# Half B's last gate and up products as 2x2 blocks: seven block products in place of eight

## The chip, the cores and the metric

The kernel runs on one core of a Trainium2 chip, as one launch. The metric is the device time of a run in microseconds (us); lower is better. A core has five engines that run their own queues in order and meet at semaphores: PE (TensorE, matmuls; PEld is its weight load), DVE (VectorE), ACT (ScalarE), POOL (GpSimd) and SP (SyncE), from whose queue the DMAs of this kernel are issued. SBUF is the on-chip memory of 128 partitions, PSUM the memory of eight banks into which PE writes.

## The reference

Two layers work on 1088 tokens of 1024 channels: 1024 of a prompt, 64 of a running stream. Layer 0 mixes tokens by two recurrences (an RWKV-7 state and a gated linear attention), layer 1 by attention over the own chunk of 64 tokens and the eight before it. After each comes a layer norm, then a channel mixer and another layer norm:

```python
def swiglu(x, w_in, w_out):
    gate, up = jnp.split(x @ w_in, 2, axis=-1)
    return (jax.nn.silu(gate) * up) @ w_out

x = layer_norm(DEEPNORM_ALPHA * x + mix, P['ln1_w'][layer], P['ln1_b'][layer])
x = layer_norm(DEEPNORM_ALPHA * x + swiglu(x, P['ffn_w_in'][layer], P['ffn_w_out'][layer]),
               P['ln2_w'][layer], P['ln2_b'][layer])
```

`FFN_HIDDEN` is 2816, so `x @ w_in` has 5632 columns, 2816 of gate and 2816 of up. Everything is fp32, and the outputs are the two sequences and the states.

## The kernel before, in words

The tokens are two halves: A with 448 (384 of the prompt and the 64 of the stream), B with the other 640. Every stage exists once per half, and stages of the two halves are interleaved, so that PE has matmuls while the other engines work on the other half. A scheduler of the framework sets the order of each engine's queue from the program, its dependencies and its own estimate of the times; pools of a fixed number of buffers (`bufs`) set how far work can run ahead.

Precision comes from splitting: a value is kept as a high part `hi` (fp32r) and a low part `lo` (what the rounding left), and a product of two split values takes three matmuls, hi*hi, hi*lo and lo*hi. `split` (L108) makes both from an fp32 source, the high part by a copy on ACT (L110), the low part by a subtraction on DVE (L111). `load_w` (L91) does the same for a weight tile of 512 KB: DMA into `wr` (two buffers), cast on ACT (L98) into `wh`, low part into `wl`, in the later stages 5/8 on DVE (L103) and 3/8 on POOL (L105); `wh` and `wl` have four buffers each.

`layer_norm` (L847) works on one tile of 128 tokens at a time: statistics and scaling on DVE, ACT and POOL (L861 to L874), then eight transposes on PE (L879) into two PSUM banks of four blocks, and a split of each bank into `xt`, the normalised tokens with channels on the partitions: `xh` and `xl`, eight blocks of 128 channels by 640 tokens for half B. `proj` (L840) is the product ahead of that norm, and calls it for each token tile.

`ffn` (L891) is the channel mixer. It goes over 22 hidden tiles `j` of 128. For each it loads the gate's and the up's weights (`w_fi`, eight blocks of 128x128 each), and `gemm_ws` (L113) makes for each of them and for both segments of 320 tokens 24 matmuls of 320 columns: 96 for a tile. Three PSUM banks (`bank`, L136) turn round. Tanh on ACT (L903) and two steps on DVE (L904, L908) give silu(gate) * up, which is split into `hh` and `hl` (L912, L914). After the 4th, 8th, 12th, 16th, 18th and 22nd hidden tile `tsg` (L792) multiplies those hidden tiles with the output weights (`w_fo`) and adds to the token accumulators `acc` on DVE (L814, L816). With the last group each finished token tile goes through its layer norm.

`run` (L1162) strings this together. Near the end `proj` and the first layer norm of half B in layer 1 run within half A's mixer (after its hidden tile 20); then follows the rest of half A's mixer with its last layer norm, whose tiles go out to memory; then half B's mixer and last norm, to the end.

## Time and profile before

| | us |
|---|---|
| median of three runs | 3122.81 (3121.77 to 3125.4) |
| profiled execution | 3121.55 |
| its span, first to last instruction | 3119.8 |
| half B's first norm of layer 1, from its statistics on | 2588.27 |
| first gate matmul of half B's last mixer | 2646.90 |
| last matmul | 3108.2 |

The profile is of one execution. A row of a timeline has the start in us, the duration in us, engine, source line, operation and the tiles written and read, then in brackets the engine's idle time ahead of it and what ended that. A row of a grouped view has the summed duration and the mean in ns. The view of stretches has for each engine the busy time and the count of instructions, then the clock granted to PE as a share of the full one, the DMA share and GB/s. Matmul ends are modelled and overlap, so the distance between starts is their rate.

### The profile page before, as it was taken

The page shows a single profiled execution, that of the slowest core. Times are in us where ns is not written, and L with a number is a line of the kernel's source. Part 1 is how long each engine was busy: PE and PEld are TensorE (multiplying, and loading weights), DVE is VectorE, ACT ScalarE, POOL GpSimd, SP SyncE. Part 2 cuts the span into 40 slices and gives each one's busy share as a digit, 9 for nine tenths or more (in the row PEclk, how much of TensorE's full clock was granted, in tenths as well). Part 3 has the DMA queues.
Part 4 walks back from the last instruction along what each step waited for, and adds up shares of the span by engine and source line. Part 5 has one row for each costly group of instructions (what it writes and reads, how often), then busy time and mean ns, then how long its engine had stood idle before and what let it go on. Part 6 is the DMA issues. An engine that isn't in the chain of part 4 may idle for free.

```text
span 3119.8 us, 50207 instructions
## 1 busy us (share of the span) xinstructions
PE 3038.1 (97%) x17732; PEld 2705.3 (87%) x17732; DVE 1898.4 (61%) x4786; ACT 1208.7 (39%) x2657; POOL 1228.6 (39%) x1373
## 2 busy tenths in 40 slices
PE   8999999799999999999999999999999999999998
PEld 7788888688888878888999898899999988999997
DVE  5677875878899764375554466254666668433345
ACT  4454554344454323334442132354444442222221
POOL 2354533444455233343342233244455544222222
PEclk9989999889999999999999999999999999999999
DMA  6554434533533238534442233866454543322221
GB/s 208 139 156 113 109 110 122 147 103 106 148 109 107 87 104 270 179 99 125 119 129 92 81 95 104 249 185 185 132 142 136 148 140 108 106 81 69 82 75 68
DMA packets 297338, 395.10 MB, mean 127 GB/s; under 512 B 125376, under 2 KB 218424, under 8 KB 297088
## 3 DMA queue, kind: packets, MB, share of 16 engines
q1 hardware_dynamic: 297088, 391.90, 42.3%
q8 instruction: 140, 2.29, 0.3%
q14 instruction: 110, 0.90, 0.1%
HBM read 319.44 MB, written 75.51 MB: 127 GB/s over the span
## 4 chain that ended last, share of the span: by engine, by line
PE 83%; DVE 8%; DMA 5%; issue 2%; ACT 1%; POOL 1%; SPq 1%; POOLq 0%; DVEq 0%; ACTq 0%
PE gps L121 14%; PE gps L122 14%; PE gps L123 14%; PE gps L131 8%; PE gps L132 8%; PE gps L134 8%; PE op L1150 2%; PE tp L1124 2%; PE sps L1108 1%; DVE t L541 1%; DVE x L543 1%; PE sps L1109 1%; PE ps L614 1%; DVE wl L103 1%; PE pb L476 1%
## 5 line engine op out<-in xcount | busy, mean ns | idle before, releaser
L121 PE MATMUL gps<-xh,wh 128*128 128x320 f32 (+1 forms) x2892 | 963.0, 333 | 8.2 <-ACT xh L207 5.9
L122 PE MATMUL gps<-xl,wh 128*128 128x320 f32 (+1 forms) x2892 | 961.9, 333 | 0.6 <-DVE xl L208 0.6
L123 PE MATMUL gps<-xh,wl 128*128 128x320 f32 (+1 forms) x2892 | 959.2, 332 | 1.0 <-DVE wl L103 0.9
L105 POOL TENSOR_TENSOR wl<-wr,wh 128x384 fp32r<-128x384 f32 (+2 forms) x333 | 577.3, 1738 | 904.6 <-ACT wh L98 859.0
L98 ACT CAST wh<-wr 128x1024 fp32r<-128x1024 f32 x396 | 413.2, 1048 | 707.4 <-issue 234.9
L121 PEld LDWEIGHTS gps<-xh,wh 128*128 128x128 f32 x2892 | 545.7, 189 | 30.2 <-ACT xh L207 5.9
L123 PEld LDWEIGHTS gps<-xh,wl 128*128 128x128 f32 x2892 | 545.0, 188 | 19.5 <-DVE wl L103 2.1
L122 PEld LDWEIGHTS gps<-xl,wh 128*128 128x128 f32 x2892 | 545.2, 189 | 18.4 <-DVE xl L208 1.0
L103 DVE TENSOR_TENSOR wl<-wr,wh 128x640 fp32r<-128x640 f32 (+2 forms) x333 | 319.2, 959 | 339.8 <-ACT wh L98 338.0
L1119 POOL TENSOR_SCALAR s<-s,mx 128x640 f32<-128x640 f32 (+5 forms) x144 | 203.0, 1410 | 289.0 <-DVE mx L1118 249.6
L131 PE MATMUL gps<-wh,hh 128*128 128x512 f32 x792 | 313.0, 396 | 0.6 <-DVE acc L816 0.6
L132 PE MATMUL gps<-wl,hh 128*128 128x512 f32 x792 | 311.6, 395 | 0.0
L134 PE MATMUL gps<-wh,hl 128*128 128x512 f32 x704 | 274.3, 395 | 2.6 <-DVE hl L914 2.6
L816 DVE TENSOR_TENSOR acc<-acc,gps 128x512 f32<-128x512 f32 (+1 forms) x216 | 145.2, 681 | 105.9 <-PE gps L134 100.5
L134 PE MATMUL gps<-wh,xl 128*128 128x512 f32 (+1 forms) x441 | 175.9, 403 | 4.8 <-DVE xl L208 4.8
L131 PE MATMUL gps<-wh,xh 128*128 128x512 f32 (+1 forms) x441 | 176.0, 405 | 4.3 <-DVE acc L814 3.5
L132 PE MATMUL gps<-wl,xh 128*128 128x512 f32 (+1 forms) x441 | 176.6, 403 | 2.8 <-DVE wl L103 2.8
L131 PEld LDWEIGHTS gps<-wh,hh 128*128 128x128 f32 x792 | 149.2, 189 | 32.4 <-DVE acc L816 3.3
L541 DVE TENSOR_TENSOR t<-lt,x 16x48 f32<-16x48 f32 (+9 forms) x540 | 151.0, 280 | 40.7 <-DMA lt<-l_d 30.3
L908 DVE SCALAR_TENSOR_TENSOR ht<-ht,gps 128x320 f32<-128x320 f32 (+1 forms) x132 | 69.8, 529 | 173.8 <-PE gps L123 173.7
L132 PEld LDWEIGHTS gps<-wl,hh 128*128 128x128 f32 x792 | 149.3, 189 | 29.1 <-DVE wl L103 0.3
L1117 ACT ACTIVATE s<-s,mx 128x640 f32<-128x640 f32 (+5 forms) x144 | 96.5, 670 | 178.7 <-DVE mx L1116 174.8
(288 smaller groups left out, 4945.3 us busy)
## 6 DMA issues: line engine op xcount, KB each, us to landing
wr<-in_w_fi SPq DMA_DIRECT2D x176, 512.0 KB
wr<-in_w_fo SPq DMA_DIRECT2D x88, 512.0 KB
wr<-in_w_in SPq DMA_DIRECT2D x44, 512.0 KB
wr<-in_w_qk SPq DMA_DIRECT2D x32, 512.0 KB
qs<-qd SPq DMA_DIRECT2D x32, 320.0 KB
wr<-in_w_om SPq DMA_DIRECT2D x16, 512.0 KB
wr<-in_w_v SPq DMA_DIRECT2D x16, 512.0 KB
vd<-vh SPq DMA_DIRECT2D x16, 512.0 KB
```

The costliest lines, as they stand in the source:

```text
L98: self.A.copy(hi, raw)
L103: self.V.tensor_tensor(lo[:, :h], raw[:, :h], hi[:, :h].bitcast(F32), op=ALU.subtract)
L105: self.G.tensor_tensor(lo[:, h:], raw[:, h:], hi[:, h:].bitcast(F32), op=ALU.subtract)
L121: self.T.matmul(ps, hi[:, kt, :], xh, start=(kt == 0), stop=False)
L122: self.T.matmul(ps, hi[:, kt, :], xl, start=False, stop=False)
L123: self.T.matmul(ps, lo[:, kt, :], xh, start=False, stop=(kt == nk - 1))
L131: self.T.matmul(ps, hi(kt)[:, cols], wh, start=(i == 0), stop=False)
L132: self.T.matmul(ps, hi(kt)[:, cols], wl, start=False, stop=(lo is None and i == n - 1))
L134: self.T.matmul(ps, lo(kt)[:, cols], wh, start=False, stop=(i == n - 1))
L541: V.tensor_tensor(tv, lt[:, j, w:16].unsqueeze(2).to_broadcast([m, r, w]), x[:, 0, j, 0:w].unsqueeze(1).to_broadcast([m, r, w]), op=ALU.mult)
L816: self.V.tensor_tensor(a, a, ps[:m], op=ALU.add)
L1119: G.tensor_scalar(s[:m, :nk], s[:m, :nk], mx[:m, 3:4], None, op0=ALU.mult)
```

## The change

The change rewrites the gate and up product of half B's mixer in layer 1, and nothing else of the arithmetic. The input x of 640 tokens by 1024 channels is seen as 2x2 blocks: A11 and A12 are the first 320 tokens with channels 0 to 511 and 512 to 1023, A21 and A22 the other 320 tokens. The weights of a hidden tile are 2x2 blocks as well: B11 and B21 the two channel halves of the gate, B12 and B22 those of the up. Of these are made

- from x: S1 = A21 + A22, S2 = S1 - A11, S3 = A11 - A21, S4 = A12 - S2
- from the weights: T1 = B12 - B11, T2 = B22 - T1, T3 = B22 - B12, and T4 = B21 - T2,

and the results come from the seven products A11\*B11, S2\*T2, S1\*T1, S3\*T3, A12\*B21, S4\*B22 and A22\*T4, with sums between them. Each product has four channel blocks with three matmuls of 320 columns, 12, so a tile has 84.

The S blocks are made in `layer_norm` (`s_operands`): for each pair of 64-token chunks, one of each token half, DVE recovers blocks from their parts (hi + lo), adds and subtracts, and each block is split with a copy on ACT and a subtraction on DVE. A21 stands in S1's place until its sum is made. The token tiles are taken in the order 2, 0, 3, 1, 4. The transposed blocks of a token tile stay in their two PSUM banks until both its chunks are done. The T blocks are made per hidden tile (`s_weights`): POOL makes four differences of 512 columns in place in `wr`, ACT casts 3.5 tiles of 1024 columns for the 2 of before, and DVE makes all low parts. The weight buffers turn between the former ones, one pair in the mixer's own pool, and the four tiles that held half A's accumulators (whose rows leave for memory by SP's queue, in which the next weight loads are issued too). The partial results pa, pb and pc occupy the three PSUM banks through a whole hidden tile; between products ACT and DVE read them (c1, c2, c3). `hh` and `hl` lie in half A's `xt`, which is free by then.

```diff
-    def layer_norm(self, hf, acc, which, layer, out=None, transpose=True):
+    def layer_norm(self, hf, acc, which, layer, out=None, transpose=True, sums=None):
...
-                    self.split(xt.hi[:, ks, ts], xt.lo[:, ks, ts], p3)
+                    if sums is None:
+                        self.split(xt.hi[:, ks, ts], xt.lo[:, ks, ts], p3)
+                    else:
+                        halves.append(p3)
+            if sums is not None:
+                sums(i, *halves)
...
+        def chunk(q, p):
+            cs = slice(64 * (q % 5), 64 * (q % 5) + 64)
+            own, other = (("A11", "A12"), ("S1", "A22"))[:: 1 if q < 5 else -1]
+            here = (q + 5) % 10 in held
+            for n, src in zip(own, p):
+                if n != "S1" or not here:
+                    put(n, cs, src)
+            if not here:
+                held.add(q)
+                return
...
+            c, s, t = tmp_("sc"), tmp_("ss"), tmp_("st")
+            if q < 5:
+                a11, a12 = p
+                back("S1", c)
+                V.tensor_tensor(s, c, back("A22", t), op=ALU.add)
+            else:
+                a11, a12 = back("A11", t), None
+                A.copy(c, p[0])
+                V.tensor_tensor(s, p[1], c, op=ALU.add)
+            put("S1", cs, s)
+            V.tensor_tensor(c, a11, c, op=ALU.subtract)
+            put("S3", cs, c)
+            V.tensor_tensor(s, s, a11, op=ALU.subtract)
+            put("S2", cs, s)
+            V.tensor_tensor(s, a12 or back("A12", t), s, op=ALU.subtract)
+            put("S4", cs, s)
...
+    def s_weights(self, j, layer, turn):
...
+        put(("B11", "B21"), g)
+        G.tensor_tensor(g[:, b1], u[:, b1], g[:, b1], op=ALU.subtract)
+        G.tensor_tensor(u[:, b1], u[:, b2], u[:, b1], op=ALU.subtract)
+        put(("B22",), u[:, b2])
+        G.tensor_tensor(u[:, b2], u[:, b2], g[:, b1], op=ALU.subtract)
+        put(("T3", "T2"), u)
+        G.tensor_tensor(g[:, b2], g[:, b2], u[:, b2], op=ALU.subtract)
+        put(("T1", "T4"), g)
...
+    def s_ffn(self, layer, acc, x, hp, hidden, turn, after):
...
+            product(pa, "A11", "B11", True)
+            c1 = tmp("c1")
+            A.copy(c1, pa)
+            product(pb, "S2", "T2", True)
+            c2 = tmp("c2")
+            V.tensor_tensor(c2, pb, c1, op=ALU.add)
+            product(pc, "S1", "T1", True)
+            product(pb, "S3", "T3", False)
+            c3 = tmp("c3")
+            V.tensor_tensor(c3, pb, c1, op=ALU.add)
+            V.tensor_tensor(c3, pc, c3, op=ALU.add)
+            product(pa, "A12", "B21", False)
+            A.activation(t1, pa, AF.Tanh, scale=0.5)
+            V.scalar_tensor_tensor(t1, t1, 1.0, pa, op0=ALU.add, op1=ALU.mult)
+            product(pc, "S4", "B22", False)
+            V.tensor_tensor(c2, pc, c2, op=ALU.add)
+            G.tensor_tensor(t1, t1, c2, op=ALU.mult)
+            product(pb, "A22", "T4", False)
+            V.tensor_tensor(c1, pb, c1, op=ALU.add)
+            A.activation(t2, c1, AF.Tanh, scale=0.5)
+            V.scalar_tensor_tensor(t2, t2, 1.0, c1, op0=ALU.add, op1=ALU.mult)
+            G.tensor_tensor(t2, t2, c3, op=ALU.mult)
...
+        def turn(kind, dt):
+            n = turns[kind]
+            turns[kind] += 1
+            if kind == "wr":
+                pool, tag, bufs = ((self.wp, "wr", 2), (accA, "acc", 4))[n // 2 % 2]
+            else:
+                pool, tag, bufs = (((self.wp, kind, self.WB),) * 4 + ((hp, kind, 1), (accA, "acc", 4)))[n % 6]
+            return pool.tile([128, 8, 128], dt, tag=tag, name=kind, bufs=bufs)
```

The scheduler's order moves with it. The first place is PE's queue at the seam of half A's mixer and half B's. Before, the last matmuls with output weights (`hh`) run straight into the first gate product:

```order
13071 L132 MATMUL gps<-wl,hh 128x512
13072 L121 MATMUL gps<-xh_27957,wh 128x320 [waits DVE_49,Activation_49]
13073 L122 MATMUL gps<-xl_27958,wh 128x320
13074 L123 MATMUL gps<-xh_27957,wl 128x320
13075 L121 MATMUL gps<-xh_27957,wh 128x320
```

Now the last token tile's second four transposes stand between them; then come A11 (from 13072), A12 (from 13084), and at 13096 the first matmul with S2, whose low part is first read at 13116 and which S3 follows at 13132:

```order
13069 L134 MATMUL gps<-wl,hh 128x512
13070 L884 MATMUL tps<-ident,acc 128x128 [waits DVE_49,PE_49]
...
13072 L1039 MATMUL gps<-xh_27957,wh 128x320 [waits DVE_49,Activation_49]
...
13084 L1039 MATMUL gps<-xh_27957,wh 128x320 [waits Activation_49]
...
13096 L1039 MATMUL gps<-S2h,wh 128x320 [waits DMAHW3_49,DMAHW2_49,DMAHW4_49,PE_49,Activation_49]
...
13116 L1040 MATMUL gps<-S2l,wh 128x320 [waits DVE_49]
...
13132 L1039 MATMUL gps<-S3h,wh 128x320 [waits DVE_49]
```

So two products stand ahead of the first one that needs sums of all token tiles.

The second place is DVE's queue at the same seam. Before, the tail of half A's norm (`acc`) is followed by the weights and the gate of half B's first hidden tile:

```order
4428 L103 TENSOR_TENSOR wl<-wr,wh 128x640 [waits DMAHW3_49,Activation_49]
4429 L861 BN_STATS bs<-acc 64x6 [waits DVE_49]
4430 L904 SCALAR_TENSOR_TENSOR ht<-ht,gps 128x320 [waits Activation_49]
4431 L863 BN_AGGR mv<-bs 64x2 [waits DVE_49]
4432 L869 SCALAR_TENSOR_TENSOR acc<-acc,mv,gb 64x512 [waits DVE_49]
```

Now the end of that norm is followed by the sums of the last chunk (`ss`, `sc`, `st` are the temporaries, `xl` holds S1's low part) and by one weight block of the second hidden tile, before the low part of S2 is complete:

```order
4480 L879 SCALAR_TENSOR_TENSOR acc<-acc,rstd,gb 64x512 [waits DVE_49,Pool_49]
4481 L992 TENSOR_TENSOR ss<-st,ss 128x256 [waits DVE_49]
4482 L975 TENSOR_TENSOR st<-xh_27957,xl_27958 128x256 [waits DVE_49]
4483 L112 TENSOR_TENSOR S4l<-ss,S4h 128x4x64 [waits Activation_49]
4484 L986 TENSOR_TENSOR ss<-tps,sc 128x256 [waits DVE_49]
4485 L988 TENSOR_TENSOR sc<-st,sc 128x256 [waits DVE_49]
4486 L1014 TENSOR_TENSOR wl<-wr,wh 128x512 [waits DMAHW7_49,DMAHW3_49,Pool_49]
4487 L112 TENSOR_TENSOR xl_27958<-ss,xh_27957 128x4x64 [waits Activation_49]
4488 L112 TENSOR_TENSOR S3l<-sc,S3h 128x4x64 [waits Activation_49]
4489 L990 TENSOR_TENSOR ss<-ss,st 128x256 [waits DVE_49]
4490 L975 TENSOR_TENSOR st<-xh_27957,xl_27958 128x256 [waits DVE_49]
4491 L112 TENSOR_TENSOR S2l<-ss,S2h 128x4x64 [waits Activation_49]
```

In the rows from the second pair of statistics of half B's norm (4344) to this one there are 36 low parts of 256 columns (L112), 29 sums and differences (L975 to L992), and four low parts of weights of 1024 and two of 512 (L1014).

The third place is DVE's queue in the middle of a group of hidden tiles. Before, a weight's low part of 640 columns stands between steps on the gate:

```order
4438 L914 TENSOR_TENSOR hl<-ht,hh 128x640 [waits Activation_49]
4439 L904 SCALAR_TENSOR_TENSOR ht<-ht,gps 128x320 [waits Activation_49]
4440 L103 TENSOR_TENSOR wl<-wr,wh 128x640 [waits DMAHW7_49,PE_49,Activation_49]
4441 L904 SCALAR_TENSOR_TENSOR ht<-ht,gps 128x320 [waits Activation_49]
4442 L908 SCALAR_TENSOR_TENSOR ht<-ht,gps 128x320 [waits DVE_49,PE_49] x2
```

Now low parts of 1024 and 512 stand between the rows that read the banks (`gps`):

```order
4564 L1057 TENSOR_TENSOR c_29756<-gps,c_29716 128x320 [waits PE_49]
4565 L1058 TENSOR_TENSOR c_29756<-gps,c_29756 128x320 [waits DVE_49]
4566 L1014 TENSOR_TENSOR wl<-wr,wh 128x1024 [waits DMAHW6_49,Activation_49]
4567 L1014 TENSOR_TENSOR wl<-wr,wh 128x1024 [waits PE_49,Activation_49]
4568 L1061 SCALAR_TENSOR_TENSOR ht<-ht,gps 128x320 [waits Activation_49]
4569 L1066 TENSOR_TENSOR c_29716<-gps,c_29716 128x320 [waits PE_49]
4570 L1014 TENSOR_TENSOR wl<-wr,wh 128x512 [waits DMAHW7_49,Activation_49]
4571 L1063 TENSOR_TENSOR c_29730<-gps,c_29730 128x320 [waits PE_49]
```

A bank is thus emptied behind up to two low parts of weights.

More of the change, by code (lines that the diff above doesn't have):

```diff
@@ L926, in ffn, with s_operands, put, tmp_ @@
             yield j
+    def s_operands(self, pool, tmp):
+        V, A = self.V, self.A
+        hi, lo = self.xt[1].hi, self.xt[1].lo
+        H = slice(0, 320), slice(320, 640)
+        K = slice(0, 4), slice(4, 8)
+        x = {"A11": [(t[:, K[0], H[0]]) for t in (hi, lo)], "A12": [(t[:, K[1], H[0]]) for t in (hi, lo)],
+             "A22": [(t[:, K[1], H[1]]) for t in (hi, lo)], "S1": [(t[:, K[0], H[1]]) for t in (hi, lo)]}
+        for n in ("S2", "S3", "S4"):
+            x[n] = [pool.tile([128, 4, 320], F32R, name=n + p, tag=n + p) for p in "hl"]
+        held = set()
+        def put(n, cs, src):
+            self.split(x[n][0][:, :, cs], x[n][1][:, :, cs], src)
+        def chunk(q, p):
[8 more added lines that the diff above has]
+                return
+            def tmp_(n):
+                return tmp.tile([128, 4, 64], F32, tag=n, name=n, bufs=1)
+            def back(n, t):
+                V.tensor_tensor(t, x[n][0][:, :, cs].bitcast(F32), x[n][1][:, :, cs].bitcast(F32), op=ALU.add)
+                return t
+            c, s, t = tmp_("sc"), tmp_("ss"), tmp_("st")
[14 more added lines that the diff above has]
+            put("S4", cs, s)
+        def sums(i, p1, p2):
+            for e in range(2):
+                chunk(2 * i + e, [p[:, :, 64 * e : 64 * e + 64] for p in (p1, p2)])
+        return x, sums
@@ new lines, in s_weights, with put @@
+    def s_weights(self, j, layer, turn):
+        V, A, G, nc = self.V, self.A, self.G, self.nc
+        B = {}
+        g, u = (turn("wr", F32) for _ in range(2))
+        for t, c in ((g, j), (u, NHT + j)):
+            nc.sync.dma_start(t, self.a["w_fi"][layer, c])
+        b1, b2 = slice(0, 4), slice(4, 8)
+        def put(names, src):
+            m = src.shape[1]
+            hi, lo = turn("wh", F32R)[:, :m], turn("wl", F32R)[:, :m]
+            A.copy(hi, src)
+            V.tensor_tensor(lo, src, hi.bitcast(F32), op=ALU.subtract)
+            for i, n in enumerate(names):
+                B[n] = hi[:, 4 * i : 4 * i + 4], lo[:, 4 * i : 4 * i + 4]
+        put(("B11", "B21"), g)
[6 more added lines that the diff above has]
+        put(("T1", "T4"), g)
+        return B
@@ new lines, in s_ffn, with product, tmp @@
+    def s_ffn(self, layer, acc, x, hp, hidden, turn, after):
+        V, A, G, T = self.V, self.A, self.G, self.T
+        hs, done = {}, 0
+        for j in range(NHT):
+            B = self.s_weights(j, layer, turn)
+            pa, pb, pc = (self.bank()[:, :320] for _ in range(3))
+            def product(ps, xn, bn, first):
+                (xh, xl), (wh, wl) = x[xn], B[bn]
+                for kt in range(4):
+                    T.matmul(ps, wh[:, kt, :], xh[:, kt, :], start=(first and kt == 0), stop=False, skip_group_check=True)
+                    T.matmul(ps, wh[:, kt, :], xl[:, kt, :], start=False, stop=False, skip_group_check=True)
+                    T.matmul(ps, wl[:, kt, :], xh[:, kt, :], start=False, stop=(kt == 3), skip_group_check=True)
+            def tmp(n, w=320):
+                return hp.tile([128, w], F32, tag=n, name=n, bufs=2)
+            t = tmp("ht", 640)
+            t1, t2 = t[:, :320], t[:, 320:]
+            product(pa, "A11", "B11", True)
[20 more added lines that the diff above has]
+            G.tensor_tensor(t2, t2, c3, op=ALU.mult)
+            hh, hl = hidden(j)
+            A.activation(hh, t, AF.Copy, scale=0.5)
+            V.scalar_tensor_tensor(hl, t, 0.5, hh.bitcast(F32), op0=ALU.mult, op1=ALU.subtract)
+            hs[j] = hh, hl
+            end = j + 1
+            if end in self.GROUPS:
+                self.tsg(1, acc, lambda nh, pr: self.a["w_fo"][layer, nh, pr], range(done // 2, end // 2),
+                         lambda kt: hs[kt][0], lambda kt: hs[kt][1], done == 0, after() if end == NHT else None)
+                for i in range(done, end):
+                    del hs[i]
+                done = end
@@ L1266, in run @@
             next(f)
-        acc0 = self.load_acc(0, self.x_d, self.ctx.enter_context(tc.tile_pool(name="accA1", bufs=1, side="right")))
+        accA = self.ctx.enter_context(tc.tile_pool(name="accA1", bufs=1, side="right"))
+        acc0 = self.load_acc(0, self.x_d, accA)
         with tc.tile_pool(name="xs", bufs=1, side="right") as xsp:
```

43 lines of the change are left out of this document (26 added, 17 removed).

## The prediction

> **What bounds the kernel now.** I read the page first: engine shares, then the chain that ended last.
>
> ```profile
> PE 3038.1 (97%) x17732; PEld 2705.3 (87%) x17732; DVE 1898.4 (61%) x4786; ACT 1208.7 (39%) x2657; POOL 1228.6 (39%) x1373
> PE 83%; DVE 8%; DMA 5%; issue 2%; ACT 1%; POOL 1%; SPq 1%; POOLq 0%; DVEq 0%; ACTq 0%
> ```
>
> TensorE bounds the kernel, so fewer matmuls count in full only where PE is busy and stays busy. The stages that the change touches, by the view of busy time per stretch:
>
> ```profile
> core 0: us, PE busy (x) PEld busy (x) DVE busy (x) ACT busy (x) POOL busy (x), PEclk, DMA share, GB/s
> 2594.00:2656.00 62.00, 62.00 (x320) 53.56 (x318) 61.08 (x91) 23.04 (x32) 35.85 (x34) 1.00 0.31 113
> 2656.00:2748.00 92.00, 92.00 (x563) 87.02 (x562) 36.96 (x53) 21.57 (x28) 26.87 (x17) 1.00 0.32 99
> 2748.00:3088.00 340.00, 339.69 (x2062) 320.39 (x2062) 125.11 (x174) 74.23 (x99) 81.33 (x48) 1.00 0.23 73
> 3088.00:3120.00 32.00, 20.56 (x90) 16.47 (x89) 25.64 (x40) 3.62 (x5) 12.01 (x15) 0.90 0.21 82
> ```
>
> Two things stand there. From 2656 to 3088, half B's last mixer, PE is never idle and DVE is busy 40% at most: matmuls saved there are saved time. But in the 62 us ahead of it (LN of half B, then the end of half A's mixer with its own LN) DVE is full too, 61.08 of 62. PE does not notice, because its next work needs only half B's LN, long done. The change puts new DVE work into just this stretch and makes PE wait for it.
>
> **The products.** The order on PE shows 84 matmuls of 320 columns per hidden tile where 96 stood. Their price is the distance between starts, not the recorded duration:
>
> ```profile
> 2646.68 0.39 PE L132 MATMUL gps<-wl,hh 128*128 128x512 f32 x1
> 2646.90 0.31 PE L121 MATMUL gps<-xh,wh 128*128 128x320 f32 x1
> 2647.05 0.31 PE L122 MATMUL gps<-xl,wh 128*128 128x320 f32 x1
> 2647.20 0.31 PE L123 MATMUL gps<-xh,wl 128*128 128x320 f32 x1
> 2647.34 0.31 PE L121 MATMUL gps<-xh,wh 128*128 128x320 f32 x1
> ```
>
> Three in 0.44 us are 0.147 us each. 12 fewer in each of 22 tiles are 264, so **-38.7 us**. A product of 12 lasts 1.76 us, a tile's seven 12.3 us. The second product of the mixer (matmuls with wo) keeps its count, and so does the tail after 3088.
>
> **The wait for the sums.** On PE the new stage issues 24 matmuls (A11, A12), then S2 with all its 320 columns, which come from all five token tiles. DVE works in order, so S2 is there when DVE has finished the row of S2l (the last row of the DVE piece shown with the change). I count its queue from a point that both kernels share:
>
> ```profile
> 2593.75 1.28 DVE L861 BATCH_NORM_STATS2 bs<-acc 128x6 f32<-128x512 f32 x2
> 2608.86 0.67 DVE L816 TENSOR_TENSOR acc<-acc,gps 128x512 f32<-128x512 f32 x1
> 2609.45 0.68 DVE L111 TENSOR_TENSOR xl<-tps,xh 128x512 fp32r<-128x512 f32 x1
> 2654.50 1.12 DVE L103 TENSOR_TENSOR wl<-wr,wh 128x640 fp32r<-128x640 f32 x1
> L111 DVE TENSOR_TENSOR xl<-tps,xh 128x256 fp32r<-128x256 f32 x6 | 2.4, 410 | 2.2 <-ACT xh L110 2.2
> L103 DVE TENSOR_TENSOR wl<-wr,wh 128x1024 fp32r<-128x1024 f32 x63 | 78.3, 1243 | 48.7 <-ACT wh L98 48.4 <-issue 0.2
> DVE acc L816 <- PE gps L134: 3.8, 2, 3.5
> ```
>
> From 2593.75 to the end of the row at 2654.50, 2655.6, DVE waits for almost nothing (the last row: 3.8 us from 2592 to 2656, nearly all ahead of it). Starts in a row are 0.59 us apart where 0.68 is recorded, so I take 0.08 off each duration: 0.60 for 512 columns, 0.33 for 256, 1.16 for 1024. Against those 61.9 us the queue up to S2l has
>
> - 36 low parts of 256 (11.9) for 10 of 512 (6.0): +5.9
> - 29 sums and differences of 256: +9.6
> - the split of the first tile's weights and one of the second's, four of 1024 and two of 512 (5.8), for the four of 640 in that stretch (3.5): +2.3
> - the rest of half A's LN, which now stands ahead of S2: four rows of 512 at 0.65 and one of 0.2, +2.8.
>
> That is 20.6 us, and S2 at 2676. To this come hand-offs: 20 of the new low parts wait for a copy on ACT that itself waits for the sum on DVE; the row of 256 shows 2.2/6 = 0.37 us idle ahead of each, up to 7.4 us. And 8 new differences of 512 on POOL, 1.30 us each by the first row below, can hold DVE up to 10.4 us:
>
> ```profile
> 2601.70 1.30 POOL L872 TENSOR_TENSOR acc<-acc,gb 128x512 f32<-128x512 f32 x1 [1.23 <-ACT acc L871]
> 2774.08 0.70 DVE L103 TENSOR_TENSOR wl<-wr,wh 128x512 fp32r<-128x512 f32 x1 [0.49 <-ACT wh L98]
> 2774.71 1.90 DVE L914 TENSOR_TENSOR hl<-ht,hh 128x640 fp32r<-128x640 f32 x1
> 2774.13 1.79 POOL L105 TENSOR_TENSOR wl<-wr,wh 128x512 fp32r<-128x512 f32 x1 [5.24 <-ACT wh L98]
> ```
>
> L914 takes 1.90 and ends 0.7 after POOL's row: it seems to stand until POOL is done. Together 0 to 18 us; part of both is filled by half A's LN rows in between, and I take 8. S2 is ready at 2684. PE's 24 matmuls, started at 2646.90 as now, would be through at 2650.4. So PE loses **+33.7 us** (25.7 to 43.7) at the seam, the term that eats the gain. A gain is excluded: PE gets no work that it could do earlier. Behind the waiting S2 stands everything on PE, the second tile's A11 too.
>
> **The clock after the wait.** PE will stand for tens of us.
>
> ```profile
> 1360.00:1370.00 10.00, 4.86 (x27) 4.59 (x26) 6.95 (x15) 3.02 (x7) 3.67 (x4) 0.83 0.56 190
> 620.00:630.00 10.00, 7.87 (x35) 6.35 (x36) 9.87 (x29) 4.09 (x12) 5.40 (x9) 0.50 0.41 129
> ```
>
> After a stand of some 5 us the clock is 0.83 in the 10 us of the restart, 1.7 us lost; in broken work it was 0.50 for 10 us. Dense products follow here, as in the first row: **+2 us** (0 to 5). The Trainium skill ("TensorE: Matmul & The Clock Gate", Part 1) has half clock for a window of about 3.4 us after an idle one, an estimate of 1.7 us; the first row agrees.
>
> **Inside the groups.** Per tile ACT casts 3.5 blocks of 1024 instead of 2, DVE makes all low parts, POOL makes four differences and two products instead of low parts.
>
> ```profile
> L98 ACT CAST wh<-wr 128x1024 fp32r<-128x1024 f32 x64 | 67.3, 1051 | 289.0 <-issue 163.1 <-PE gps L122 65.8 <-PE gps L134 52.9
> L908 DVE SCALAR_TENSOR_TENSOR ht<-ht,gps 128x320 f32<-128x320 f32 x44 | 21.5, 488 | 93.3 <-PE gps L123 93.3
> L903 ACT ACTIVATE ht<-gps 128x320 f32<-128x320 f32 x44 | 19.1, 435 | 44.7 <-PE gps L123 44.7
> L912 ACT CAST hh<-ht 128x640 fp32r<-128x640 f32 x22 | 15.9, 722 | 0.0
> ```
>
> ACT: 3.5 x 1.05 + 3 x 0.43 + 0.72 = 5.7 us; DVE: 3 x 1.16 + 0.60 + 7 x 0.41 + 0.73 = 7.7; POOL: 4 x 1.30 + 2 x 0.8 = 6.8 (320 columns scaled from 512). PE has 12.3, so each is hidden on average, and 27 us of matmuls with wo after every fourth tile let weights run ahead. Loads stay at two of 512 KB per tile. What can show: pa, pb and pc hold all three banks, so each emptying on DVE has one product, 1.76 us, and a low part of 1.16 or a POOL row of 1.30 may stand before it. A miss costs nothing up to 1.2 us per tile (1.30 + 1.16 + 0.41 + hand-off against 1.76). Most emptyings need 0.41 of 1.76, so I take 0.3 per tile, **+6 us** (0 to 26). If that cover goes, it is TensorE that stands.
>
> **Sum.** The profiled execution took 3121.55 us (span 3119.8): 3121.55 - 38.7 + 33.7 + 2 + 6 = 3124.6. It lies 1.3 us under the median of 3122.81, so 3125.8 beside that; I say **3125 us**, no change that can be told.
>
> **Rivals.**
>
> The sums cost their bare queue. The order interleaves them with half A's LN, so hand-offs and POOL find other rows to hide behind; against it stands that the last two chunks come after that LN and have only each other. Then S2 is at 2676, the restart costs 1.7, tiles nothing: 3121.55 - 38.7 + 25.7 + 1.7 = 3110 us, 3111.6 beside the median, faster.
>
> The weights become the bound inside the groups. If DVE rows with both inputs in SBUF and POOL rows exclude each other, as the row of 1.90 suggests, a tile has 4.1 + 0.73 + 0.41 on DVE and 6.8 on POOL in a line, 12.0 of PE's 12.3, and each difference waits for a low part and feeds the next. For it: four dependent POOL steps per tile. Against it: the room after every fourth tile. At 1.2 us per tile it gives 3121.55 - 38.7 + 33.7 + 2 + 26 = 3145 us, 3146 beside the median, slower. It decides from 0.42 us per tile on: without tiles the sum is 3118.6, 3119.9 beside the median, and 9.2 us more over 22 tiles pass 3129. The Trainium skill ("SBUF — State Buffer", "SBUF: two separate sides") says that the two engines share a port pair under an exclusive lock held for a whole instruction; by that rule the line of 12.0 is real and this rival is the one it speaks for. L914's 1.90 agrees, the 0.70 of L103 beside a running POOL row is the side that came first.
>
> Or the change doesn't cut the matmuls. The order on PE says that it does; time as before, 3123.
>
> **How the numbers follow.** Forecast 0.45 (its own range 3116 to 3133; 0.37 of it within 0.2%, 0.08 above), bare queue 0.25, weights bound 0.27, no cut 0.03. A change of 0.2%, 6.2 us, is about what a measurement of this kernel tells from none. Faster is the bare queue, 0.25; same 0.37 + 0.03 = 0.40; slower 0.27 + 0.08 = 0.35. The range goes from just under the bare queue, 3108, to the weights bound, 3144; full gain without any wait (3083) and the sum of all upper bounds (3157) are left out.
>
> **What would show it.** In the changed profile: matmuls of 320 in half B's last mixer 0.147 us apart and 264 fewer; one PE wait of 25 to 44 us behind the first 24 of them, released by DVE or ACT on S2; DVE full from 2594 to that release; a clock below 1 right after; in the groups PE idle under 0.5 us per tile, released by DVE rows that empty banks. It is wrong if PE stands under 20 us at the seam (the queue was not the limit), or if the idle time is spread over the tiles.

## The result and the profile after

| | before | after |
|---|---|---|
| median, us | 3122.29 (4 runs, 3116.81 to 3125.4) | 3149.84 (4 runs, 3147.94 to 3153.79) |
| profiled execution, us | 3121.55 | 3148.22 |
| its span | 3119.8 | 3146.1 |
| first gate matmul of half B's last mixer | 2646.90 | 2651.31 |
| last matmul | 3108.17 | 3134.54 |

The change makes the kernel slower: ratio 1.0092, 95% interval 1.0074 to 1.011. The forecast was no change, and the time lies 6 us over its range.

The page of the changed kernel, engine shares and the chain that ended last:

```profile
PE 3012.1 (96%) x17468; PEld 2670.6 (85%) x17468; DVE 2026.2 (64%) x4953; ACT 1264.6 (40%) x2753; POOL 1331.3 (42%) x1461
PE 73%; DVE 12%; DMA 7%; issue 3%; ACT 2%; POOL 2%; SPq 1%; POOLq 0%; DVEq 0%; ACTq 0%
```

264 matmuls are gone (17468 for 17732), and TensorE's share of the chain fell from 83% to 73%: it is made to wait. Where, the view of stretches tells (columns as in the prediction):

```profile
2594.00:2651.00 57.00, 54.52 (x260) 45.01 (x259) 56.52 (x108) 22.25 (x43) 23.29 (x26) 1.00 0.25 84
2651.00:2688.00 37.00, 10.18 (x43) 8.89 (x42) 34.38 (x50) 12.49 (x23) 21.01 (x15) 0.59 0.37 121
2688.00:3106.00 418.00, 399.10 (x2344) 366.79 (x2343) 254.87 (x322) 137.60 (x185) 195.27 (x142) 1.00 0.23 75
3106.00:3146.00 40.00, 28.60 (x130) 23.24 (x129) 31.11 (x46) 6.83 (x9) 18.01 (x20) 0.91 0.20 79
```

There are two losses: 27 us of 37 at the seam, while DVE is full, and 19 us of 418 behind it, where before almost nothing was idle. TensorE's timeline at the seam:

```profile
2651.31 0.39 PE L1039 MATMUL gps<-xh,wh 128*128 128x320 f32 x1
2654.52 0.63 PE L1041 MATMUL gps<-xh,wl 128*128 128x320 f32 x1 [2.67 <-DVE wl L1014]
2659.86 0.41 PE L1040 MATMUL gps<-xl,wh 128*128 128x320 f32 x1 [1.38 <-DVE xl L112]
2661.55 0.47 PE L1041 MATMUL gps<-xh,wl 128*128 128x320 f32 x1
2684.26 0.64 PE L1039 MATMUL gps<-S2h,wh 128*128 128x320 f32 x1 [22.25 <-DVE st L975]
2684.70 0.47 PE L1039 MATMUL gps<-xh,wh 128*128 128x320 f32 x1
2684.97 0.47 PE L1040 MATMUL gps<-xl,wh 128*128 128x320 f32 x1
...
2688.65 0.31 PE L1039 MATMUL gps<-xh,wh 128*128 128x320 f32 x1
2688.80 0.31 PE L1040 MATMUL gps<-xl,wh 128*128 128x320 f32 x1
```

After 24 matmuls it stands 22.25 us for S2, then starts at 0.27 us per matmul for 4.2 us. The view names L975 as the releaser; what the matmul reads is the cast of S2h, which follows the sum L990. The rows of DVE and ACT just ahead:

```profile
2680.89 1.48 DVE L112 TENSOR_TENSOR S3l<-sc,S3h 128x256 fp32r<-128x256 f32 x1
2682.30 1.48 DVE L990 TENSOR_TENSOR ss<-ss,st 128x256 f32<-128x256 f32 x1
2683.81 0.40 ACT L111 CAST S2h<-ss 128x256 fp32r<-128x256 f32 x1 [4.48 <-DVE ss L990]
```

So it is a wait for the last sum. The first 24 matmuls were late too: they start 3.0 us later than before the change and take 10.7 us instead of 3.5, since they wait for a weight's low part (2.67), start 0.27 us apart behind it, and wait for the low part of A12 (1.38). Behind S2, the view of waits (2690 to 3146: total, times, longest):

```profile
PE gps L1039 <- DVE ht L1061: 4.3, 5, 1.2
PE gps L1041 <- DVE wl L1014: 3.4, 5, 0.7
PE gps L133 <- ACT xh L1071: 2.5, 3, 1.6
PE gps L1039 <- DVE c L1057: 2.1, 4, 0.6
PE gps L1039 <- ACT wh L1013: 2.1, 2, 1.8
PE gps L133 <- DVE acc L818: 1.9, 5, 0.6
```

They are small and many: rows that empty banks (L1061, L1057), weights' low parts (L1014) and casts (L1013), hidden parts (L1071). The busy share understates them, since modelled ends overlap. So for this and all runs below I take **the loss**, from the one profiled execution of each run: the distance from the first gate matmul to the last matmul, less 0.1467 us per matmul of 320 columns and 0.2268 per one of 512 (spacings in dense rows). Before it is 1.8 us; after, 29.4 up to the first matmul with S2 and 33.0 behind it. From the second pair of statistics rows of half B's norm (before 2593.75, after 2595.12) the last matmul comes 25.0 us later than before:

- first gate matmul 56.2 us behind those rows, not 53.2: +3.0
- 264 matmuls: -38.7
- loss up to S2: +29.4
- loss behind it, 33.0 less 1.8: +31.2, of which 1.8 is the slow restart.

With 1.4 us of drift ahead and 0.3 at the tail these are the 26.7 us between the two executions.

### The profile page after: what moved, and what is told of

Read it like the earlier page. It is cut to its first block, busy times and chain, and to the rows that moved or that the text cites. A ratio compares the mean times of both kernels' runs of the same rounds, so it can differ in the third digit from the quotient of the medians.

```text
span 3146.1 us, 50008 instructions
## 1 busy us (share of the span) xinstructions
PE 3012.1 (96%) x17468; PEld 2670.6 (85%) x17468; DVE 2026.2 (64%) x4953; ACT 1264.6 (40%) x2753; POOL 1331.3 (42%) x1461
## 4 chain that ended last, share of the span: by engine, by line
PE 73%; DVE 12%; DMA 7%; issue 3%; ACT 2%; POOL 2%; SPq 1%; POOLq 0%; DVEq 0%; ACTq 0%
PE gps L122 11%; PE gps L123 11%; PE gps L124 11%; PE gps L133 7%; PE gps L134 7%; PE gps L136 6%; PE gps L1039 2%; PE op L1304 2%; PE gps L1040 2%; PE gps L1041 2%; PE tp L1278 2%; DVE t L543 1%; DVE wl L104 1%; DVE x L545 1%; PE sps L1262 1%
## 5 line engine op out<-in xcount | busy, mean ns | idle before, releaser
L106 POOL TENSOR_TENSOR wl<-wr,wh 128x512 fp32r<-128x512 f32 (+2 forms) x289 | 506.0, 1755 | 626.5 <-ACT wh L99 580.5
L122 PE MATMUL gps<-xh,wh 128*128 128x320 f32 (+1 forms) x2188 | 748.4, 342 | 10.2 <-ACT xh L209 5.7
L123 PE MATMUL gps<-xl,wh 128*128 128x320 f32 (+1 forms) x2188 | 747.2, 341 | 0.6 <-DVE xl L210 0.6
L124 PE MATMUL gps<-xh,wl 128*128 128x320 f32 (+1 forms) x2188 | 744.1, 340 | 0.7 <-DVE wl L104 0.7
L122 PEld LDWEIGHTS gps<-xh,wh 128*128 128x128 f32 x2188 | 415.3, 190 | 32.0 <-ACT wh L99 6.0
L104 DVE TENSOR_TENSOR wl<-wr,wh 128x512 fp32r<-128x512 f32 (+2 forms) x289 | 284.5, 985 | 244.0 <-ACT wh L99 239.4
L133 PE MATMUL gps<-wh,xh 128*128 128x512 f32 x661 | 262.6, 401 | 10.9 <-DVE acc L816 4.0
L136 PE MATMUL gps<-wh,xl 128*128 128x512 f32 x661 | 259.5, 398 | 4.8 <-DVE xl L210 4.8
L134 PE MATMUL gps<-wl,xh 128*128 128x512 f32 x661 | 261.7, 398 | 2.0 <-DVE wl L104 2.0
L818 DVE TENSOR_TENSOR acc<-acc,gps 128x512 f32<-128x512 f32 (+1 forms) x216 | 144.7, 679 | 85.3 <-PE gps L136 79.8
L545 DVE TENSOR_TENSOR x<-x,t 16x48 f32<-16x48 f32 (+9 forms) x540 | 144.0, 267 | 10.9
```

The lines of the kernel that those rows point to most:

```text
L104: self.V.tensor_tensor(lo[:, :h], raw[:, :h], hi[:, :h].bitcast(F32), op=ALU.subtract)
L106: self.G.tensor_tensor(lo[:, h:], raw[:, h:], hi[:, h:].bitcast(F32), op=ALU.subtract)
L122: self.T.matmul(ps, hi[:, kt, :], xh, start=(kt == 0), stop=False)
L123: self.T.matmul(ps, hi[:, kt, :], xl, start=False, stop=False)
L124: self.T.matmul(ps, lo[:, kt, :], xh, start=False, stop=(kt == nk - 1))
L133: self.T.matmul(ps, xh, wh, start=(i == 0), stop=False)
```

## The experiments

Medians in us, the kernel before on the same chip beside them; losses from each profile. With plain tiles first the loss is given whole.

| run | median | before | ratio, 95% | loss to S2 / behind |
|---|---|---|---|---|
| the change | 3149.84 | 3122.29 | 1.0074 to 1.011 | 29.4 / 33.0 |
| e1 no sums | 3129.51 | 3120.43 | 1.0015 to 1.0035 | 5.7 / 43.3 |
| e2 no differences | 3131.61 | 3120.43 | 1.0017 to 1.0045 | 25.2 / 20.6 |
| e3 differences on DVE | 3138.29 | 3120.43 | 1.0041 to 1.0071 | 27.6 / 27.0 |
| e4 six banks | 3146.0 | 3120.43 | 1.0066 to 1.01 | 25.8 / 33.0 |
| e5 norm four tiles earlier | 3163.65 | 3121.52 | 1.012 to 1.0163 | 7.6 / 45.5 |
| e6 idle differences | 3144.83 | 3121.52 | 1.0059 to 1.01 | 31.4 / 32.7 |
| e7 POOL out | 3141.95 | 3121.52 | 1.0045 to 1.0092 | 27.5 / 33.0 |
| e8 = e5 with e7 | 3154.82 | 3121.52 | 1.0077 to 1.0136 | 10.9 / 35.8 |
| e9 three plain tiles | 3129.93 | 3121.14 | 1.0018 to 1.0039 | 37.6 |
| e10 = e9 with e3 | 3120.46 | 3121.14 | 0.9987 to 1.0009 | 27.3 |
| e11 two plain tiles, e3 | 3126.2 | 3121.14 | 1.0006 to 1.003 | 40.4 |
| e12 norm two tiles earlier, e3 | 3131.43 | 3121.14 | 1.0017 to 1.0044 | 10.5 / 31.2 |
| e13 no low parts | 3120.55 | 3123.33 | 0.9983 to 1.0004 | 23.8 / 12.6 |
| e14 four plain, late sums, e3 | 3121.82 | 3123.33 | 0.998 to 1.0003 | 27.4 |
| e15 three plain, late sums, e3 | 3121.02 | 3123.33 | 0.9982 to 1.0003 | 29.9 |
| e16 sums behind the norm | 3120.81 | 3119.28 | 0.9994 to 1.0018 | 33.7 |
| e17 differences shared | 3122.14 | 3119.28 | 0.9997 to 1.0023 | 37.0 |
| **e18 sums between plain tiles** | **3108.76** | 3121.37 | **0.9955 to 0.9982** | 20.3 |

**The seam: e1.**

```diff
-                self.proj(1, acc1, "w_o", self.layer_norm(1, acc1, "ln1", 1, sums=sums))
+                self.proj(1, acc1, "w_o", self.layer_norm(1, acc1, "ln1", 1)); xs.update(S2=xs["A11"], S3=xs["S1"], S4=xs["A12"])
```

> Left out: all sums of token blocks. S2, S3 and S4 are read from A11, A21 and A12, so the product counts on TensorE stay, and half B's norm splits its blocks as before the change. Every theory says that the 33.9 us at the seam are a wait for the sums: S2 ready at 2684.3 against the 2650.4 at which TensorE would reach it, plus some 2 us of slower clock after it. If these 36 us are lost to nothing but the wait, the time is 3150 - 36 = 3114 us (3109 to 3119), and the 29 us lost after the seam stay. If the wait at the seam hides work that TensorE would wait for anyway (weights of the first tiles), less comes back: 3125 or more.

The wait for S2 is gone and the first gate matmul is back at 53.4 us behind the norm's statistics, as before the change; but of 36 us only 16 to 20 came back (20 by the medians, 16 from those statistics to the last matmul of the profiles). From 2645 on TensorE waits there:

```profile
PE gps L1039 <- ACT wh L1013: 11.4, 5, 4.5
PE gps L1039 <- DVE ht L1061: 4.3, 5, 1.2
PE gps L1041 <- DVE wl L1014: 4.2, 6, 0.8
```

The casts of block weights cost 11.4 where they cost 2.1 in the change: while TensorE stood, these weights could run ahead. The seam's net price is 16 to 20 us.

**The groups: e2, e3, e4, e6, e7, e13.** e2 drops the four POOL lines of `s_weights`; e3 writes `V.` for `G.` in them:

```diff
-        G.tensor_tensor(g[:, b1], u[:, b1], g[:, b1], op=ALU.subtract)
+        V.tensor_tensor(g[:, b1], u[:, b1], g[:, b1], op=ALU.subtract)
```

> Left out: the four differences of weight blocks per hidden tile on POOL (T blocks are the raw blocks); casts, low parts, loads and products keep their counts. Lock theory (DVE rows with both inputs in SBUF and POOL rows exclude each other, a tile's line of 12.0 us falls to 6.8): the 29 us after the seam fall to 8 or less, and the seam gets some 4 us shorter: 3116 to 3128 us. Bank theory (emptyings of three banks stand behind low parts in DVE's order): the 29 us stay nearly whole: 3138 to 3150. Buffer theory (casts wait for a free weight buffer or a load): the same, 3138 to 3150, perhaps some 5 less since a load's buffer is released sooner.

> Nothing left out: the four differences per tile move from POOL to DVE, 0.6 us each there against 1.3. Lock theory: a tile's line of exclusive work falls from 12.0 to some 9.2 us, so the 29 us after the seam fall to some 10; at the seam 8 x 0.6 more on DVE stand against the lock's waits there: 3125 to 3135 us. Bank theory: DVE has 2.4 us more per tile ahead of the emptyings: 3150 to 3175, slower than the change as it is. Buffer theory: about 3150.

Without the differences 20.6 us of 33.0 stay, where the lock theory allowed 8: POOL's rows are a part, not the whole. On DVE they cost half of that gain back. The groups of rows from 2690 to 3105 show how POOL reaches DVE. The change:

```profile
L1014 DVE TENSOR_TENSOR wl<-wr,wh 128x1024 fp32r<-128x1024 f32 x61 | 82.2, 1352 | 51.3 <-ACT wh L1013 48.1 <-PE gps L1041 3.0
L1014 DVE TENSOR_TENSOR wl<-wr,wh 128x512 fp32r<-128x512 f32 x20 | 24.0, 1202 | 3.0 <-issue 1.9 <-ACT wh L1013 1.1
L1072 DVE SCALAR_TENSOR_TENSOR xl<-ht,xh 128x640 fp32r<-128x640 f32 x21 | 22.0, 1048 | 19.9 <-ACT xh L1071 19.7
L1068 DVE SCALAR_TENSOR_TENSOR ht<-ht,c 128x320 f32<-128x320 f32 x21 | 21.5, 1025 | 3.8 <-ACT ht L1067 3.8
L1057 DVE TENSOR_TENSOR c<-gps,c 128x320 f32<-128x320 f32 x22 | 10.7, 488 | 18.0 <-PE gps L1041 17.9
```

and without the differences:

```profile
L1014 DVE TENSOR_TENSOR wl<-wr,wh 128x512 fp32r<-128x512 f32 x20 | 15.9, 797 | 3.2 <-issue 1.9 <-ACT wh L1013 1.3
L1068 DVE SCALAR_TENSOR_TENSOR ht<-ht,c 128x320 f32<-128x320 f32 x22 | 18.0, 818 | 4.3 <-ACT ht L1067 4.3
L1057 DVE TENSOR_TENSOR c<-gps,c 128x320 f32<-128x320 f32 x21 | 10.3, 489 | 25.5 <-PE gps L1041 25.3
```

Rows with both inputs in SBUF get shorter when POOL does less (1202 to 797 ns, 1025 to 818); the row that reads a bank takes 488 and 489. At the seam it shows row by row: S3l and L990, shown above, take 1.48 us each, beside POOL rows of 1.31 and 1.32 that start 0.11 and 0.13 us ahead of them; other rows of their kind take 0.41. The Trainium skill ("SBUF — State Buffer", "SBUF: two separate sides") names this case, a DVE row with two SBUF inputs against a POOL row that reads SBUF; the trace agrees.

e4 gives every second tile the transposes' banks:

```diff
-            pa, pb, pc = (self.bank()[:, :320] for _ in range(3))
+            pa, pb, pc = ((self.tpsum() if j % 2 else self.bank())[:, :320] for _ in range(3))
```

> Nothing left out: every second hidden tile takes its three banks from the three that the transposes leave free, so a tile's products never wait for the emptying of the tile before. Bank theory: the stalls that end with the emptying rows (L1061, L1057, L1063, some 13 of the 29 us) go, and the emptyings are no longer urgent: 3130 to 3138 us. Lock theory: rows still take as long and the line of 12.0 us per tile stays, though slack is larger: 3140 to 3150. Buffer theory: stalls move to the casts and low parts of weights: 3143 to 3150.

Most of the bank waits go, and the loss behind S2 stays at 33.0, because others take their place:

```profile
PE gps L133 <- ACT xh L1071: 12.8, 5, 4.3
PE gps L1039 <- DVE c L1053: 2.2, 2, 1.3
```

The banks were only where DVE's lateness surfaced; now the hidden parts for the second product come late. At the seam the extra banks let 24 matmuls of the second tile run ahead of S2 as well, and the loss there falls by 3.6 us. e6 keeps POOL busy with rows that nothing reads, e7 also moves L1064 and L1069 to DVE:

```diff
-        G.tensor_tensor(g[:, b1], u[:, b1], g[:, b1], op=ALU.subtract)
+        G.tensor_tensor(self.scr, g[:, 0:3].rearrange("p k t -> p (k t)"), g[:, 4:7].rearrange("p k t -> p (k t)"), op=ALU.subtract)
```

> Left out: the four differences of weight blocks, as in the run without them; but POOL still has four rows per tile of 384 columns (1.0 us each, three quarters of the time) with both inputs in SBUF, whose result nothing reads. Lock theory (the rows cost time because they and DVE's exclude each other): most of the 13 us that the run without differences gained after the seam is lost again, 28 us or more stand there, and 3 of the 7 at the seam: 3138 to 3148 us. Chain theory (the differences cost time because casts wait for them one after the other): as without them, 3127 to 3134.

> Nothing left out: the four differences and the two products per tile move from POOL to DVE, so that POOL keeps only a half of the low parts of the output weights. Lock theory: the two products' rows (0.87 alone) no longer lengthen DVE's rows, and hidden parts come sooner: under 20 us after the seam against 27 with the differences alone moved: 3126 to 3133 us. Load theory (what counts is how full DVE is: 7.7 us per tile in the sum, here 10.9): more than 27 us there: 3139 to 3150.

Rows without a reader cost as much as the real ones (32.7), so it is not that casts wait for differences; nor is it a weight buffer held longer, since TensorE waits for no cast in e6 from 2690 on. The largest wait there is on hidden parts,

```profile
PE gps L133 <- ACT xh L1071: 7.3, 3, 3.3
```

whose two products queue on POOL behind those rows: lock and POOL's own order are not told apart by it. And with POOL nearly quiet (e7) the loss is 33.0 again, as the load theory has it. L1014 of 512 columns is back at 684 ns there, so more rows in DVE's queue cost as much as stretched ones. Of the 6 us over e3, some 5 are waits for the additions to `acc` (L816, L818: 7.5 us, in e3 2.7). DVE's mean load does not order the runs: from 2690 to 3090 it is busy 244 of 400 us in the change and 280 in e3, which loses 6 us less. e13 takes the other half:

```diff
-            V.tensor_tensor(lo, src, hi.bitcast(F32), op=ALU.subtract)
...
-                B[n] = hi[:, 4 * i : 4 * i + 4], lo[:, 4 * i : 4 * i + 4]
+                B[n] = hi[:, 4 * i : 4 * i + 4], hi[:, 4 * i : 4 * i + 4]
```

> Left out: the low parts of the block weights (3.5 rows of 1024 columns per tile on DVE); TensorE reads the high parts in their place, so its counts stay; the differences stay on POOL. Theory of two halves (a tile's weights cost on DVE and on POOL, in one line by the lock; the 20 us that stayed without differences are bank emptyings and hidden parts queued behind these low parts): with POOL's half alone nothing is left to queue behind, the loss after the seam falls from 33 to under 10, and the seam is some 7 us shorter: 3108 to 3120 us. If what stays is the order of products, the group ends or the number of banks: 18 us or more are lost after the seam, 3125 to 3140.

12.6 us are left, a little over the 10 expected, with all of POOL's rows in place; some 1.5 of them are the slow restart. The largest waits that stay are those at the group ends:

```profile
PE gps L133 <- ACT xh L1071: 2.1, 2, 1.9
PE gps L133 <- DVE acc L818: 1.6, 5, 0.3
```

So of 33 us taking out the low parts gives back 20, and taking out the differences 12. TensorE's own waits for these low parts are 3.4 us in the change, so most of the 20 comes through what is queued behind them. No run leaves out both, so it is not shown that the two add. How they do it shows on DVE in the change at 2722:

```profile
2722.58 1.62 DVE L1068 SCALAR_TENSOR_TENSOR ht<-ht,c 128x320 f32<-128x320 f32 x1 [0.54 <-ACT ht L1067]
2724.12 0.48 DVE L1063 TENSOR_TENSOR c<-gps,c 128x320 f32<-128x320 f32 x1
2724.52 3.53 DVE L1014 TENSOR_TENSOR wl<-wr,wh 128x1024 fp32r<-128x1024 f32 x2
2727.97 1.77 DVE L104 TENSOR_TENSOR wl<-wr,wh 128x512 fp32r<-128x512 f32 x1
2729.67 0.47 DVE L1061 SCALAR_TENSOR_TENSOR ht<-ht,gps 128x320 f32<-128x320 f32 x1
```

with POOL at the same time:

```profile
2722.55 1.30 POOL L1024 TENSOR_TENSOR wr<-wr 128x512 f32<-128x512 f32 x1
2725.12 1.85 POOL L1064 TENSOR_TENSOR ht<-ht,c 128x320 f32<-128x320 f32 x1
2726.93 2.27 POOL L106 TENSOR_TENSOR wl<-wr,wh 128x512 fp32r<-128x512 f32 x1
```

TensorE's rows that waited meanwhile:

```profile
2726.30 0.41 PE L1041 MATMUL gps<-S2h,wl 128*128 128x320 f32 x1 [0.68 <-DVE wl L1014]
2730.20 0.50 PE L133 MATMUL gps<-wh,xh 128*128 128x512 f32 x1 [0.36 <-DVE ht L1061]
```

L1068 stands until POOL's row ends at 2723.85; three low parts, alternating with POOL, take 5.2 us; the emptying L1061 is queued behind them, and TensorE waits for a low part and then for the bank.

**Another place for the sums: e5, e8, e12.** One number: half B's norm after half A's tile 16 (e5, e8) or 18 (e12). e8 has e7's edit as well: the differences and also the two products are on DVE, where its expectation left the products on POOL. e12 has e3's.

```diff
-        self.HB, self.PRE, self.JO, self.JM = 5, 4, 16, 20
+        self.HB, self.PRE, self.JO, self.JM = 5, 4, 16, 16
```

> Nothing left out: half B's first norm with its sums starts after half A's hidden tile 16 instead of 20, so that DVE makes the sums while TensorE still has five tiles of half A's mixer. Seam theory (TensorE stands because the sums are late on a full DVE): S2's last row now comes 52 rows of DVE ahead of the end of half A's norm instead of 9 behind it, so the wait of 22.6 us is gone and with it the slower clock after it. What comes back is not the whole 36 us: without sums at all 12 us of the weights' waits took the seam's place, and half A's last norm still stands ahead of the first emptyings: 3118 to 3130 us. If the wait were for something else at that place (the weights of the first tile, half A's norm), it stays: 3145 to 3155.

> Nothing left out: half B's norm after half A's hidden tile 16, and the differences on DVE (POOL keeps the two products). If seam and groups are two losses that add, this has the gain of both: 3150 less 12 for the differences less the gain of the earlier norm (20 to 32): 3106 to 3118 us, faster than the kernel before. If the loss in the groups grows when the seam's wait no longer lets the weights run ahead, as in the run without sums, 3118 to 3126.

> Nothing left out, no plain tiles: half B's norm after half A's hidden tile 18 (not 20, and not 16 as in the run that lost), differences on DVE. The norm starts some 19 us earlier. If the 24 us that the earlier norm cost ahead of the seam come from running into the end of half B's attention, two tiles keep most of that distance, and the wait shrinks from 21 us to a few: 3118 to 3126 us. If each tile earlier costs what it saves: 3136 to 3145.

e5 has no wait for sums (S2's matmul waits 2.6 us for a cast), yet the first gate matmul comes at 2675.47, 24 us later. e5's stretch at the end of half B's attention, where the change has 50.00 of 50:

```profile
2500.00:2550.00 50.00, 37.91 (x154) 30.66 (x153) 19.01 (x38) 16.15 (x30) 18.27 (x11) 0.73 0.37 132
```

TensorE is idle for 12 of the 50 us, at a granted clock of 0.73; its longest wait there is 6.9 us for the attention's output to be loaded (`xh`, L209). By the program's order, the mixer tiles that had filled this place are now behind the norm. e8 comes to 3154.82, 9 us under e5 (e7 gained 8 on the change) and far from either expectation, which were for another edit. Two tiles earlier (e12) gain 7 us on e3, between the two that were expected: the loss up to S2 falls by 17.1 us, the one behind it grows by 4.2, and the first gate matmul comes later, so of the 17 us some 7 stay.

**Work in the seam's place: e9 to e11, e14 to e18.** The first hidden tiles of half B are computed as before the change, S1 is made once they are done:

```diff
+            if j < 3:
+                self.plain(j, layer, hp, hidden, hs)
+                continue
+            if j == 3:
+                self.last()
```

> Nothing left out: half B's first three hidden tiles are computed as before the change, with eight products (288 matmuls of 320 columns, 42 us, that need no sums); A21 keeps its place until they are done, then S1 is made there; the block form begins at the fourth tile. If the seam's loss is nothing but TensorE without work while DVE makes the sums, the 34 us of waiting and 2 us of slow clock go and 3 x 1.76 us of products come back: 3150 - 36 + 5 = 3119 us (3114 to 3124), as fast as the kernel before. If the weights of the block form, which ran ahead during the wait, are late now (12 us in the run without sums): 3126 to 3134.

> Nothing left out: the same with the four differences per tile on DVE instead of POOL. The differences moved alone gave 12 us. If the two losses (seam, lock) add: 3119 - 12 = 3107 us (3102 to 3114), faster than the kernel before. If the room that the wait at the seam gave is needed: 3115 to 3125.

> Nothing left out: two tiles as before the change instead of three. They give TensorE 28 us of work where some 36 us are needed until S2 is there: a wait of 5 to 10 us comes back and 1.76 us of products are saved, so 4 to 8 us slower than with three tiles. If two tiles are enough (no wait at the first S2), 2 us faster than with three.

e9 and e10 took the second branch of their expectations: the seam's wait goes, other waits grow. e10 is level with the kernel before, and two tiles cover too little (one wait of 7.1 us for S1). In e14 and e15 the norm is as before the change and the sums are made from the stored parts, behind the plain tiles in the program. e14 is not all it says: the second product of its first four tiles was made only with the next group, from hidden buffers partly rewritten by then, so part of its output is made from rewritten values, with the same count of matmuls.

> Nothing left out: four hidden tiles with eight products; half B's norm as before the change (no sums in it, token tiles in their old order, transposes' banks emptied at once); all sums are made from the stored parts behind the plain tiles in the program; differences on DVE. With three plain tiles and the sums in the norm the first gate matmul came 10 us later than before the change, since acc and the plain tiles' banks queued behind sums on DVE. If that queue is the cause, the first gate matmul is back within 3 us of before and the time is 3120 - 8 + 2 = 3114 us (3108 to 3118), faster than the kernel before. If DVE is as full either way, since the sums need 15 more rows to recover blocks: 3119 to 3127.

> Nothing left out: the same with three plain tiles. 1.8 us less of products; the sums have 42 us instead of 56 until TensorE needs them: if they fit, 1 to 2 us faster than with four, otherwise 5 us or more slower.

No difference from e10 in either: in DVE's order many sums still stand ahead of the end of half A's norm, and a low part there (L104) held TensorE for 3.7 us. e16 to e18 have four plain tiles, with their second product as a group of its own, and the sums but S1 ahead of the third plain tile in the program. e16 ties the sums' temporaries to the plain tiles' buffers, e17 puts two of e16's differences back on POOL, e18 ties only the first chunk:

```diff
+                if q == 0:
+                    w = hp.tile([128, 640], F32, tag="ht", name="ht", bufs=2)
+                    c, s = (w[:, o : o + 256].rearrange("p (k t) -> p k t", k=4) for o in (0, 256))
```

> Nothing left out: four hidden tiles with eight products and their second product as one group, then eighteen in block form; differences on DVE. The sums' temporaries share the buffers of the plain tiles' gate (ht), so that DVE's order has the sums behind half A's last norm, beside the plain tiles. If the 5 to 10 us ahead of and in the first plain tiles of the earlier runs were the sums standing ahead of half A's norm and the first weights on DVE, the first gate matmul is back at 2647 to 2649 and nothing waits until 2690; 18 x 1.76 = 31.7 us of products are saved and some 20 us lost in the groups: 3121.5 - 32 + 21 = 3111 us (3106 to 3116), faster than the kernel before. If the sums only move the same DVE work to where block weights need it: 3118 to 3126.

> Nothing left out: as the run beside it, but of the four differences per tile two stay on DVE and two on POOL. Lock theory: two rows of 1.3 us on POOL in place of two of 0.6 on DVE make the exclusive line 1.4 us longer per tile, with DVE itself 1.2 us less busy: 2 to 6 us slower than all four on DVE. If DVE's own load decides by now, 2 to 5 us faster.

> Nothing left out: as the run with the sums behind half A's norm (e16), but only the first chunk of sums uses a buffer of the plain tiles' gate, so that the third and fourth plain tile no longer wait for the whole of the sums. In that run TensorE stood 9.7 us in the fourth plain tile for a bank behind the sums. If that wait goes and nothing takes its place: 3120.8 - 10 = 3111 us (3106 to 3115), faster than the kernel before. If the sums' DVE work comes back as other waits in the plain tiles or the first block tiles: 3117 to 3124, no difference.

e16 stood 9.7 us in its fourth plain tile for a bank whose emptying needs a buffer (`ht`) that the sums held. With that gone e18 is **faster than both**, as its first branch had it: 3108.76 us, 0.18 to 0.45% under the kernel before, 1.3% under the change. Its waits from 2586 to 3100, the largest:

```profile
PE gps L133 <- ACT xh L1089: 3.2, 2, 1.9
PE gps L1057 <- DVE ht L1079: 3.1, 4, 0.9
PE gps L133 <- DVE acc L818: 1.6, 4, 0.7
```

No wait for sums is among them. Against before: 18 tiles of 1.76 are -31.7, the loss of 20.3 less 1.8 is +18.5, the first gate matmul 54.7 us behind the statistics adds 1.5: -11.7, and the medians differ by 12.6. (The profiled execution of e18, 3101.78, is the lowest of its seven; 8.2 us of its lead come ahead of the statistics and do not belong to the change.) e17 against e16 (1.3 us, intervals overlapping) decides nothing, though the profiles' losses differ by 3.3 us the way that the lock theory has it.

## Why the prediction was wrong

**Right.** The products: 264 fewer, 38.7 us. The wait for the sums, in size: S2 was said to be ready at 2684 and was at 2684.26, and without the 1.4 us of drift the seam cost 32.4 us (3.0 and 29.4) where 33.7 stood. Its parts were in part luck. DVE's queue from the statistics to S2l took 89.6 us, for 61.9 + 20.6 + 8 = 90.5. Of the 7 us over the bare queue the differences on POOL are 4.3 (e2 takes 85.3, with a low part more in it), but the hand-offs, priced up to 7.4, are nearly nothing: DVE is idle for 1.8 us there, 0.9 before. And the single wait is 22.25 us, under the 25 to 44 that were to show it, because A11 and A12, said to start as now and run through, were late themselves. The restart: 1.8 us for the 2 said. The tail: 13.7 us behind the last matmul, 13.4 before.

**The step that failed** is "Inside the groups": "Most emptyings need 0.41 of 1.76, so I take 0.3 per tile, +6 us (0 to 26)". Measured are 29.4 us (the 31.2 less the restart's 1.8), 1.3 per tile, over the step's own upper bound of 1.2. With 29.4 for 6 the prediction's sum is 3148.0; the execution took 3148.2 (the smaller deviations, -1.3 at the seam and 1.4 of drift ahead of it, cancel). Two things were mis-sized in it.

- "Each is hidden on average" took 7.7 us of DVE per tile. The rows costed 3 x 1.16 + 0.60 for low parts, 0.41 for L1068 and 0.73 for hl, 5.2 together, take (82.2 + 24.0)/20.3 + 1.03 + 1.05 = 7.3, stretched by POOL. The stretch had been read off L914 and priced in the queue at the seam, but in the groups only for a rival.
- A miss was said to cost from nothing to 1.2 us, counting one low part and one POOL row ahead of an emptying. DVE's order already had two low parts there, and the rows at 2722 show three in line.

**The rivals.** "Weights become the bound inside the groups" gave 3146 us for a measured 3149.84: right in place and size. Its mechanism, a line of exclusive rows of 12.0 us per tile, was half of the truth. By that line e2 should have left 8 us, and 20.6 stayed; the low parts on DVE's queue weigh more (20) than POOL's differences (12). "The bare queue" and "no cut" are excluded by S2's time and the count. The first sign that was to show the forecast wrong, a stand under 20 us at the seam, did not come. The second, idle time spread over the tiles, is what came.

**What e1 adds.** The seam's 33.7 us was right as a wait, but not as a price: without the wait only 16 to 20 us came back, since the weights of the first tiles would have been late next. The prediction named nothing behind that stall.

Left open: how much of POOL's 12 us is the lock and how much its own queue, and whether the same rows on DVE, ordered so that the emptyings stand ahead of the low parts, would lose less. No run changes that order alone.

## What to carry to other kernels

Trading matmuls for elementwise work is paid on queues that are in order: price it by the longest run of rows that can stand ahead of one that frees a bank, not by an engine's mean share, and give rows with two SBUF inputs POOL's rows on top. When a wait is the price of late operands, put work that doesn't need them in its place (e18 gained some 40 us on the change: three plain tiles alone gave 20, the differences on DVE 9 more, a fourth plain tile and the order of the sums the rest) rather than start the operands earlier, where other work may need the time.
